# First stage with 1024-wide modulation products, x scaled on ScalarE, and value loads of the linear attention two levels ahead

## Chip, cores and metric

The kernel runs on one core of one Trainium2 chip. The metric is the device time of one execution in microseconds; the median of several executions is compared. Below, PE is TensorE's matmul, DVE is VectorE, ACT is ScalarE, POOL is GpSimd and SP is SyncE, which here only issues DMAs.

## The reference

Two layers of a decoder block run on x of 512 tokens by 1024 features. In each, the normed x is modulated by a vector c, projected once into four groups of heads, each group has its own kind of attention and a gate, and an output projection with a second norm is added back to x.

```python
def hybrid_layer(x, c, ln_pre, ln_post, w_ada, b_ada, w_in, w_out, ...):
    shift, scale, gate = jnp.split(jax.nn.silu(c) @ w_ada + b_ada, 3, axis=-1)
    h = rms_norm(x, ln_pre) * (1.0 + scale[:, None]) + shift[:, None]
    u = split_columns(h @ w_in)
...
    log_a = jax.nn.log_sigmoid(u['c_a'] @ gla_w_a2 + gla_b_a) / GLA_TAU
    o_c = gla_attention(heads(u['c_q'], GROUP_HEADS), heads(u['c_k'], GROUP_HEADS),
                        heads(u['c_v'], GROUP_HEADS), heads(log_a, GROUP_HEADS))
...
    y = mixed @ w_out
    return x + gate[:, None] * rms_norm(y, ln_post)
```

Group C is the gated linear attention: a state per head that decays by a gate and takes up keys times values, token after token.

## The kernel before

All data are float32. For matmuls every operand is split into a high and a low part (whi and wlo of a weight, HH and HL of the activations), and a product is three matmuls: HH with whi, HL with whi, HH with wlo. ACT makes the high part (a cast), DVE the low part (a subtraction). Weights come through tiles wraw (512 KB each); a cast whi (L475) waits for its load.

**The first stage** (`startup`, L659) makes the layer's input and the first two projections. Four tiles of x (128 tokens by 1024) come in, each as two loads of 256 KB. ACT sums the squares of each half (`sq_sum`, L421), DVE and POOL make rstd (`rstd2`: a sum L425 and a power L426), and DVE scales x (L676). Then, for each of the eight groups of 128 features, PE transposes x (`stage`, tp, L703), ACT applies scale and shift (hf, L709; HH, L710), DVE makes HL (L711), and PE multiplies (`mms`, L719 and L723, into a). Scale and shift are made on the fly by `macs` and `mod`: the weight w_mod comes in 32 tiles of 128x512 (256 KB), and DVE multiplies each with silu(c), csr, and sums along the row (L290). Two such products give 128 values, the first one passing on its sum through tmp; four give one group's shift and scale (adass, adags). The string FIRST gives the order of the first loads on SP: x a tile of x, C constants, w a tile of w_mod, P the layer's parameters, T and Q the first weight pieces, c the vector c.

**The linear attention** (`attn_c`, L811) is written as a tree of six levels, 64, 32, 16, 8, 4 and 2 tokens wide. Its values, made by the first projection, are stored to a DRAM buffer vd (L571) and loaded back, once as v (L817) and once per level in another layout as vs (L824): two loads of 128 KB per level, 12 in all, written one behind the other at the start of `attn_c`. Then follow the gate: zp (PE, L830), its logarithm in la (ACT L833 to L835, DVE L836 and L837), the running sum bp (PE, L841), its copy b (ACT, L843) and the steps from there to `level_scores` and `level_values`, level by level, the latter reading vs (L953).

Beside the attentions the rest of the projection runs, and in the background the second layer's modulation (wmod, L290) and the gate of the residual (wada with aac on DVE, L350), whose loads are put on the same SP queue (L282, L387).

**What sets the order.** Each engine works its instructions in a fixed order. A planner sets it when the program is built, from priorities, the order in the code and its own model of when operands are ready; so an edit moves instructions elsewhere too. All DMAs go through SP's one queue. The program has eight DMA semaphores that are used in turn, and a DMA on SP waits until the eighth before it has landed.

Of the kernel before, what the change touches and what calls it, by code (L numbers as in the profile page):

```python
# [20 lines left out]
TLS = False  # L21
B = dict(raw=4, w=3, mx=3, v4=5, dv=2, ad=2, qk=16, g=8, p=3, sz=4, pt=3, sm=4)
QT = QH = QL = QG = 0
QX = 60
FIRST = 'xCwPxwxwxwTQc'
XH = 2
SG, MG = 1, 2
# [154 lines left out]
def pack(inp):  # L182
# [8 lines left out]
    for l in range(DEPTH):  # L191
# [10 lines left out]
        w_gate[l] = wa[:, 2048:].reshape(8, 128, 2, 512).transpose(2, 0, 1, 3)  # L202
        w_mod[l] = wa[:, :2048].reshape(2, 512, 2, 8, 128).transpose(3, 2, 0, 4, 1)
        for i, n in enumerate(('nsa_w1_k', 'nsa_w1_v')):
# [26 lines left out]
def build(tc, A, out_d):  # L231
    nc = tc.nc
    PE, ACT, DVE, POOL, SP = nc.tensor, nc.scalar, nc.vector, nc.gpsimd, nc.sync
    with ExitStack() as ctx:
# [44 lines left out]
        def load_mod(l, n, p, tag):  # L279
# [24 lines left out]
        for ch in FIRST:  # L304
            if ch == 'C':
                SP.dma_start(out=cst[:, 0:256], in_=A['cst'][:, 0:256])
            elif ch == 'w':
                wmods.append(load_mod(0, len(wmods), qk_p, 'qk'))
            elif ch == 'P':
# [229 lines left out]

        def qk_t(name):  # L540
            return qk_p.tile([128, 512], F32, tag='qk', name=name)

# [32 lines left out]

        def qr_t(name):
            return qk_p.tile([128, 512], F32R, tag='qk', name=name)

        def fin_T(l, name, acc):
            par = pars[l]  # L580
            A0, B0 = slice(0, 64), slice(64, 128)
            if name == 'dka':

                kh, kl = qr_t('dkh'), qr_t('dkl')
                for hs in (A0, B0):
# [25 lines left out]
            elif name[0] == 'c':  # L611
                t = qk_t(name)
                ACT.activation(t, acc, AF.Copy, scale=32.0 ** -0.5 if name == 'cq' else 1.0)
                T[name] = t
            elif name[1] == 'q':

                x0, x1 = qr_t('x0'), qr_t('x1')
                ACT.copy(x0[A0], acc[A0])
# [4 lines left out]
            else:  # L623

                k0, k1, l0, l1 = qr_t('k0'), qr_t('k1'), qr_t('kl0'), qr_t('kl1')
                ACT.copy(k0[A0], acc[A0])
# [32 lines left out]
        def startup():  # L659

            tc.cur_priority -= SPX
            for i in range(4):
# [9 lines left out]
                if XF and i == 3:  # L672
                    for c in (slice(0, 128), slice(128, 1024)):
                        DVE.tensor_scalar(x_t[i][:, c], x_t[i][:, c], r, None, op0=ALU.mult)
                else:
                    DVE.tensor_scalar(x_t[i], x_t[i], r, None, op0=ALU.mult)  # L676
            tc.cur_priority += SPX
# [133 lines left out]
        def attn_c(l):  # L811
# [226 lines left out]
        def attn_b(l):  # L1038
# [108 lines left out]
        def wo_piece(l, n):  # L1147
# [218 lines left out]
```

## Time and profile before

| | before |
|---|---|
| median of 3 runs | 694.81 us (694.17 to 696.92) |
| profiled execution, its own time | 697.9 us |
| its span in the profile | 695.7 us |
| TensorE busy | 649.8 us, 93% |
| VectorE busy | 498.6 us, 72% |
| ScalarE busy | 336.8 us, 48% |
| chain that ended last | PE 58%, DVE 17%, DMA 12%, ACT 6% |
| vs<-vd, issue to landing | 24 loads of 128 KB, median 9.8 us |
| wmod<-in_w_mod, issue to landing | 64 loads of 256 KB, median 5.4 us |

The span is the part that the trace covers; the execution's own time is 2.2 us longer. Busy time is what an engine worked, and an engine that is not busy may still be the one that others wait for: the waits tell that. The chain is followed back from the last instruction, at each step to what released it.

### The profile page before, as it was taken

How to read it: one execution, taken by the hardware profiler on the slowest of the kernel's cores; microseconds unless marked ns; L12 is line 12 of the kernel's file. 1: busy time of each engine (PE TensorE's matmuls, PEld its weight loads, DVE VectorE, ACT ScalarE, POOL GpSimd, SP SyncE). 2: the span in 40 equal slices, each digit the busy share in tenths (PEclk: the TensorE clock that was granted, in tenths of full speed). 3: DMA queues.
4: the chain of work that ended last, by engine and by line, in shares of the span. 5: the costliest groups of instructions: out<-in, count | busy, mean ns of one | idle time of the engine just before them, and what ended most of it. 6: DMA issues, size and time to landing. Idle time of an engine off the chain costs nothing.

```text
span 695.7 us, 11980 instructions
## 1 busy us (share of the span) xinstructions
PE 649.8 (93%) x4460; PEld 524.5 (75%) x4460; DVE 498.6 (72%) x1291; ACT 336.8 (48%) x748; POOL 31.1 (4%) x57
## 2 busy tenths in 40 slices
PE   3999889989998999999998989899999999999996
PEld 1797766877777767779996768678777777778895
DVE  5985889666868787784598467743588878768656
ACT  5454444155565555663475244425545436435432
POOL 2000000000001100000012000000000000000000
PEclk9999999999999999999999999999999999999999
DMA  8955764657204444112642681212520021111143
GB/s 299 391 218 166 256 195 138 185 180 272 77 1 138 136 110 133 34 32 81 207 169 79 180 262 43 63 61 91 165 78 32 17 75 32 46 46 46 48 155 116
DMA packets 38163, 87.89 MB, mean 126 GB/s; under 512 B 4185, under 2 KB 7769, under 8 KB 38106
## 3 DMA queue, kind: packets, MB, share of 16 engines
q1 hardware_dynamic: 38106, 87.14, 38.7%
q8 instruction: 35, 0.57, 0.3%
q14 instruction: 22, 0.18, 0.1%
HBM read 81.88 MB, written 5.24 MB: 125 GB/s over the span
## 4 chain that ended last, share of the span: by engine, by line
PE 58%; DVE 17%; DMA 12%; ACT 6%; issue 4%; POOL 1%; SPq 1%; DVEq 0%; POOLq 0%; ACTq 0%
PE mmT L525 19%; PE yo L1169 9%; PE mmTM L536 5%; PE pT L771 5%; DMA wmod<-in_w_mod 4%; PE ob L785 3%; DMA vs<-vd 3%; DVE wlo L478 2%; DMA wraw<-in_w_in 2%; PE a L719 2%; PE yo L1216 2%; PE sc L638 2%; DVE wmod L290 2%; PE od L1007 2%; PE oa L785 2%
## 5 line engine op out<-in xcount | busy, mean ns | idle before, releaser
L525 PE MATMUL mmT<-HH,whi 128*128 128x512 f32 (+1 forms) x352 | 142.8, 406 | 1.4 <-ACT whi L475 1.4
L525 PE MATMUL mmT<-HH,wlo 128*128 128x512 f32 (+1 forms) x352 | 142.6, 405 | 0.4 <-DVE wlo L478 0.4
L525 PE MATMUL mmT<-HL,whi 128*128 128x512 f32 (+1 forms) x352 | 142.3, 404 | 0.0
L757 ACT ACTIVATE p<-p,m 128x256 f32<-128x256 f32 (+3 forms) x128 | 68.8, 538 | 66.9 <-DVE m L755 62.5
L478 DVE TENSOR_TENSOR wlo<-wraw,whi 128x1024 fp32r<-128x1024 f32 (+3 forms) x60 | 72.2, 1205 | 33.2 <-ACT whi L475 32.9
L475 ACT CAST whi<-wraw 128x1024 fp32r<-128x1024 f32 (+3 forms) x60 | 61.5, 1027 | 56.1 <-PE mmT L525 36.8
L525 PEld LDWEIGHTS mmT<-HH,wlo 128*128 128x128 f32 (+1 forms) x352 | 66.2, 188 | 16.1 <-issue 1.5
L525 PEld LDWEIGHTS mmT<-HH,whi 128*128 128x128 f32 (+1 forms) x352 | 66.4, 189 | 15.3 <-ACT whi L475 1.8
L525 PEld LDWEIGHTS mmT<-HL,whi 128*128 128x128 f32 (+1 forms) x352 | 66.4, 189 | 14.0 <-issue 1.2
L771 PE MATMUL pT<-cst,p 128*128 128x128 f32 x296 | 48.9, 279 | 6.0 <-DVE p L768 2.2
L536 PE MATMUL mmTM<-whi,HH 128*128 128x256 f32 (+1 forms) x160 | 48.6, 304 | 3.2 <-ACT HH L467 2.4
L755 DVE CUSTOM_DVE_ANT_0 p<-sc,cst 128x128 f32<-128x128 f32 (+3 forms) x96 | 44.8, 482 | 7.7 <-PE sc L639 7.3
L771 PEld LDWEIGHTS pT<-cst,p 128*128 128x128 f32 x296 | 33.3, 140 | 22.5 <-issue 11.8
L536 PE MATMUL mmTM<-whi,HL 128*128 128x256 f32 (+1 forms) x160 | 47.4, 297 | 0.4 <-DVE HL L468 0.4
L536 PE MATMUL mmTM<-wlo,HH 128*128 128x256 f32 (+1 forms) x160 | 47.2, 295 | 0.0
L1169 PE MATMUL yo<-wlo,HH 128*128 128x256 f32 x144 | 41.9, 291 | 0.0
L1169 PE MATMUL yo<-whi,HH 128*128 128x256 f32 x144 | 41.7, 290 | 0.0
L1169 PE MATMUL yo<-whi,HL 128*128 128x256 f32 x144 | 41.1, 286 | 0.0
L536 PEld LDWEIGHTS mmTM<-whi,HH 128*128 128x128 f32 x160 | 31.0, 194 | 6.1 <-ACT HH L467 3.5
L638 PE MATMUL sc<-k,x 128*128 128x128 f32 (+3 forms) x96 | 32.7, 352 | 0.5 <-DVE m L755 0.2
L778 DVE COPY pt<-pT 128x256 f32<-128x256 f32 (+3 forms) x60 | 28.4, 498 | 6.4 <-PE pT L771 5.5
L536 PEld LDWEIGHTS mmTM<-whi,HL 128*128 128x128 f32 x160 | 30.9, 194 | 1.9 <-DVE HL L468 0.9
(273 smaller groups left out, 1342.2 us busy)
## 6 DMA issues: line engine op xcount, KB each, us to landing
wraw<-in_w_in SPq DMA_DIRECT2D x52, 512.0 KB, 4.1
wmod<-in_w_mod SPq DMA_DIRECT2D x64, 256.0 KB, 5.4
wada<-in_w_gate SPq DMA_DIRECT2D x32, 256.0 KB, 3.1
wor<-in_w_out SPq DMA_DIRECT2D x12, 512.0 KB, 3.3
w<-in_w SPq DMA_DIRECT2D x8, 512.0 KB, 4.7
vs<-vd SPq DMA_DIRECT2D x24, 128.0 KB, 9.8
x<-in_x SPq DMA_DIRECT2D x8, 256.0 KB, 5.2
wor<-in_w_out SPq DMA_DIRECT2D x8, 256.0 KB, 2.9
```

What stands on the lines that cost most here:

```text
L290: DVE.tensor_tensor_reduce(wt, wt, csr[:, 512 * h:512 * h + 512], 0.5, init, ALU.mult, ALU.add, dst)
L475: ACT.copy(hi, raw)
L478: eng.tensor_tensor(out=lo, in0=raw, in1=hi, op=ALU.subtract)
L525: PE.matmul(acc[:m], a, b, start=(n == 0), stop=(n == 23))
L536: PE.matmul(acc[:, :ncol], a, b, start=(n == 0), stop=(n == 23))
L638: PE.matmul(out, q[e][:, qs], k[e][0][:, ks], start=True, stop=False)
L755: DVE.tensor_tensor_reduce(p[:, c], sc[:, c], mask, -0.125, 1e38 if sink is None else sink[0][:, es[j]:es[j] + 1], ALU.add, ALU.min, m[:, ...
L757: ACT.activation(p[:, c], p[:, c], AF.Exp, bias=m[:, j:j + 1], scale=-1.0, accum_out=lsum[:, j:j + 1])
L771: PE.transpose(tp[:, b:b + 128], p[:, b:b + 128], C('ident'))
L778: DVE.tensor_copy(dst, src)
L785: PE.matmul(o[hs, q0:q1], vt[:, kb, vc:vc + 64], PT[:, 512 * kb:512 * kb + q1 - q0], start=(first and kb == 0), stop=(last and kb == 3), s ...
L1169: PE.matmul(acc[:, :n_], a, b, start=(n == 0), stop=(n == last))
```

## The change

It has two parts. In the first stage of layer 0, two tiles of w_mod become one of 128x1024 (512 KB), with one product (L297 of the new kernel) in place of two and no tmp; there are 16 loads and 16 products. The pool of 512-wide tiles (qk, 16) becomes one of 1024-wide tiles (8), in which later users take two tiles at a time (`qk_pair`); kc moves to another pool. x is loaded whole, four loads of 512 KB; one activation of 1024 columns sums the squares (L686), and the scaling of x moves from DVE to ACT (L692). FIRST is another string. In `attn_c`, only levels 64 and 32 of vs are loaded at the start; each later level is loaded two levels ahead, when the scores of the level between have been written.

```diff
-B = dict(raw=4, w=3, mx=3, v4=5, dv=2, ad=2, qk=16, g=8, p=3, sz=4, pt=3, sm=4)
+B = dict(raw=4, w=3, mx=3, v4=5, dv=2, ad=2, qk=8, g=8, p=3, sz=4, pt=3, sm=4)
-FIRST = 'xCwPxwxwxwTQc'
-XH = 2
+FIRST = 'xPwxCxwxwTQwc'
+XH = 1
...
+        def load_mod0(n):
+
+            wt = qk_p.tile([128, 1024], F32, tag='qk', name='wmod')
+            SP.dma_start(out=wt, in_=A['w_mod'][0, n // 2, n % 2].rearrange('a p n -> (a p n)').rearrange('(p n) -> p n', p=128))
+            return wt
+
+        def mod0(n, wt, ss, gs):
+            o, ln, j = _P['bada'][0], _P['lnpre'][0], n // 2
+            DVE.tensor_tensor_reduce(wt, wt, csr, 0.5, pars[0][:, o + n:o + n + 1], ALU.mult, ALU.add, ss[:, n:n + 1])
+            if n % 2:
+                DVE.scalar_tensor_tensor(gs[:, j:j + 1], ss[:, n:n + 1], 1.0, pars[0][:, ln + j:ln + j + 1], op0=ALU.add, op1=ALU.mult)
...
-                    DVE.tensor_scalar(x_t[i], x_t[i], r, None, op0=ALU.mult)
+                    ACT.activation(x_t[i], x_t[i], AF.Copy, scale=r)
...
-                for n in range(4 * j, 4 * j + 4):
+                for n in range(2 * j, 2 * j + 2):
                     if len(wmods) <= n:
-                        wmods.append(load_mod(0, n, qk_p, 'qk'))
-                    mod(0, n, wmods[n], ss, gs)
+                        wmods.append(load_mod0(n))
+                    mod0(n, wmods[n], ss, gs)
...
-            for n, s in enumerate(LEVELS):
+
+            def load_level(n):
+                s = LEVELS[n]
                 vs = vsb[n // 3][:, 512 * (n % 3):512 * (n % 3) + 512].rearrange('p (i a n) -> p i a n', i=4, a=2)
                 vss[s] = vs
                 for e in range(2):
                     SP.dma_start(out=vs[64 * e:64 * e + 64].rearrange('p i a n -> p (i a n)'),
                                  in_=T['cvd'].rearrange('(m w r) e x -> w e m r x', w=2, r=s)[0, e])
+            load_level(0)
+            load_level(1)
...
                 nxt = level_scores(LEVELS[n + 1]) if n + 1 < len(LEVELS) else None
+                if n + 2 < len(LEVELS):
+                    load_level(n + 2)
                 level_values(s, at)
```

The planner's order around the change. First ACT at the start, from the first sum of squares (junk) to the first hf; ct is a step towards csr, whi are the first two weight pieces. Before:

```order
L421 ACTIVATE junk,ss<-x_111 128x512 [waits DMAHW1_49]
L421 ACTIVATE junk,ss<-x_111 128x512 [waits DMAHW2_49]
L337 ACTIVATE ct<-cb 128x512 [waits PE_49]
L421 ACTIVATE junk,ss<-x_119 128x512 [waits DMAHW6_49,DMAHW0_49]
L421 ACTIVATE junk,ss<-x_119 128x512 [waits DMAHW7_49]
L421 ACTIVATE junk,ss<-x_124 128x512 [waits DMAHW1_49,Activation_49]
L421 ACTIVATE junk,ss<-x_124 128x512 [waits DMAHW2_49]
L421 ACTIVATE junk,ss<-x_129 128x512 [waits DMAHW4_49,DVE_49]
L421 ACTIVATE junk,ss<-x_129 128x512 [waits DMAHW5_49]
L475 CAST whi<-wraw 128x996 [waits DMAHW7_49]
L709 ACTIVATE hf_234<-tp,adass,adags 128x512 [waits DVE_49,PE_49]
L475 CAST whi<-wraw 128x1024 [waits DMAHW0_49]
```

After the change:

```order
L686 ACTIVATE junk,ss<-x_111 128x1024 [waits DMAHW1_49]
L353 ACTIVATE ct<-cb 128x512 [waits PE_49]
L692 ACTIVATE x_111<-x_111,rstd 128x1024 [waits Activation_49,Pool_49]
L686 ACTIVATE junk,ss<-x_117 128x1024 [waits DMAHW4_49,DMAHW0_49]
L692 ACTIVATE x_117<-x_117,rstd 128x1024 [waits Activation_49,Pool_49]
L686 ACTIVATE junk,ss<-x_120 128x1024 [waits DMAHW6_49]
L692 ACTIVATE x_120<-x_120,rstd 128x1024 [waits Activation_49,Pool_49]
L686 ACTIVATE junk,ss<-x_124 128x1024 [waits DMAHW0_49,DVE_49]
L692 ACTIVATE x_124<-x_124,rstd 128x1024 [waits Activation_49,Pool_49]
L491 CAST whi<-wraw 128x996 [waits DMAHW2_49]
L491 CAST whi<-wraw 128x1024 [waits DMAHW3_49]
L725 ACTIVATE hf_214<-tp,adass,adags 128x512 [waits DVE_49,PE_49]
```

The scalings of x now stand between the sums of squares, and each waits for POOL's power; the two whi stand ahead of the first hf.

SP's queue in layer 0, from the DMAs just ahead of the loads of vs; wmod is the next layer's modulation and wraw the projection's weights. Before:

```order
L571 DMA vd<-v_tm_c 128x4x128 x2
L282 DMA wmod<-in_w_mod 128x512 x2
L824 DMA vs<-vd 64x512
L817 DMA v_633<-vd 64x4x128 x2
L824 DMA vs<-vd 64x512
L824 DMA vs<-vd 64x1x512 x10
L282 DMA wmod<-in_w_mod 128x512
L487 DMA wraw<-in_w_in 128x1024
L282 DMA wmod<-in_w_mod 128x512
L487 DMA wraw<-in_w_in 128x1024 x4
L282 DMA wmod<-in_w_mod 128x512
```

After the change:

```order
L286 DMA wmod<-in_w_mod 128x512
L842 DMA vs<-vd 64x512
L833 DMA v_575<-vd 64x4x128 x2
L842 DMA vs<-vd 64x512
L842 DMA vs<-vd 64x1x512 x2
L286 DMA wmod<-in_w_mod 128x512 x2
L503 DMA wraw<-in_w_in 128x1024 x2
L286 DMA wmod<-in_w_mod 128x512 x2
L503 DMA wraw<-in_w_in 128x1024
L842 DMA vs<-vd 64x1x512 x2
L503 DMA wraw<-in_w_in 128x1024
```

Behind the first four vs loads now stand two wmod, then two wraw; the other vs loads come later.

DVE in layer 0, from the products of wmod (with their accumulator reads) to the second la of the gate; dkl and dk are a low part of projected keys, x a copy of a projected piece of group B. Before:

```order
L290 ISA wmod,tmp<-wmod,csr,par 128x512 [waits DMAHW1_49]
L290 ISA tmp 128x1
L290 ISA wmod,adass<-wmod,csr,tmp 128x512 [waits DMAHW2_49,DVE_49]
L290 ISA adass 128x1
L587 TENSOR_TENSOR dkl<-mmT,dkh 64x512 [waits Activation_49] x2
L591 COPY ca<-mmT 16x512 [waits Pool_49]
L836 TENSOR_SCALAR la<-zp 128x512 [waits Activation_49]
L610 COPY x_700<-mmT 64x8x31 [waits PE_49]
L837 TENSOR_TENSOR la<-la,t_655 128x512 [waits DVE_49,Activation_49]
```

After the change:

```order
L306 ISA wmod,tmp<-wmod,csr,par 128x512 [waits DMAHW5_49]
L306 ISA tmp 128x1
L601 TENSOR_TENSOR dk<-mmT,dk 64x512 [waits Activation_49] x2
L605 COPY ca<-mmT 16x512 [waits Pool_49]
L306 ISA wmod,adass<-wmod,csr,tmp 128x512 [waits DMAHW4_49,DVE_49]
L306 ISA adass 128x1
L306 ISA wmod,tmp<-wmod,csr,par 128x512 [waits DMAHW5_49]
L306 ISA tmp 128x1
L856 TENSOR_SCALAR la<-zp 128x512 [waits Activation_49]
L624 COPY x_634<-mmT 64x8x31 [waits PE_49]
L857 TENSOR_TENSOR la<-la,t_589 128x512 [waits DVE_49,Activation_49]
```

Two more products, whose loads are the two behind vs, now stand between ca and la.

DVE in layer 1, at ca (the gate's input); aac are products of the residual's gate. Before:

```order
L478 TENSOR_TENSOR wlo<-wraw,whi 128x1024 [waits DMAHW0_49,PE_49,Activation_49]
L478 TENSOR_TENSOR wlo<-wraw,whi 128x1024 [waits DMAHW7_49,PE_49,Activation_49]
L587 TENSOR_TENSOR dkl<-mmT,dkh 64x512 [waits Activation_49] x2
L591 COPY ca<-mmT 16x512 [waits Pool_49]
L350 SCALAR_TENSOR_TENSOR aac<-wada,csil,aac 128x512 [waits DMAHW2_49,DVE_49]
L350 SCALAR_TENSOR_TENSOR aac<-wada,csil,aac 128x512 [waits DMAHW3_49,DVE_49]
L478 TENSOR_TENSOR wlo<-wraw,whi 128x1024 [waits DMAHW4_49,Activation_49]
L836 TENSOR_SCALAR la<-zp 128x512 [waits Activation_49]
```

After the change:

```order
L494 TENSOR_TENSOR wlo<-wraw,whi 128x1024 [waits DMAHW4_49,PE_49,Activation_49]
L494 TENSOR_TENSOR wlo<-wraw,whi 128x1024 [waits DMAHW3_49,PE_49,Activation_49]
L366 SCALAR_TENSOR_TENSOR aac<-wada,csil,aac 128x512 [waits DMAHW6_49,DVE_49]
L366 SCALAR_TENSOR_TENSOR aac<-wada,csil,aac 128x512 [waits DMAHW7_49,DVE_49]
L366 SCALAR_TENSOR_TENSOR aac<-wada,csil,aac 128x512 [waits DMAHW2_49,DVE_49]
L494 TENSOR_TENSOR wlo<-wraw,whi 128x1024 [waits DMAHW0_49,PE_49,Activation_49]
L601 TENSOR_TENSOR dk<-mmT,dk 64x512 [waits Activation_49] x2
L605 COPY ca<-mmT 16x512 [waits Pool_49]
```

Three aac now stand ahead of dk and ca, where before two stood behind ca.

## Rows read from the trace of the kernel before

**Rows 1.** page, part 1 (busy us, share, count) and part 4 (last chain).

```profile
PE 649.8 (93%) x4460; PEld 524.5 (75%) x4460; DVE 498.6 (72%) x1291; ACT 336.8 (48%) x748; POOL 31.1 (4%) x57
...
PE 58%; DVE 17%; DMA 12%; ACT 6%; issue 4%; POOL 1%; SPq 1%; DVEq 0%; POOLq 0%; ACTq 0%
```

**Rows 2.** timeline, ACT, 0 to 20: start, us, line, operation, tiles, [idle <-releaser].

```profile
4.84 0.62 ACT L421 ACTIVATE junk<-x 128x512 f32<-128x512 f32 x1
...
15.25 1.02 ACT L475 CAST whi<-wraw 128x996 fp32r<-128x996 f32 x1 [1.17 <-DMA wraw<-in_w_in]
...
18.74 0.60 ACT L710 CAST HH<-hf 128x512 fp32r<-128x512 f32 x1
```

**Rows 3.** timeline, DVE, 0 to 20 us: the last x scaling.

```profile
15.69 0.75 DVE L676 TENSOR_SCALAR x<-x,rstd 128x1024 f32<-128x1024 f32 x1 [0.44 <-POOL rstd L426]
```

**Rows 4.** timeline, POOL, 0 to 20 us: the last of four powers (rstd).

```profile
14.66 0.99 POOL L426 TENSOR_TENSOR rstd<-rstd,mhalf 128x1 f32<-128x1 f32 x1 [0.99 <-DVE rstd L425]
```

**Rows 5.** waits, PE, 0 to 52 us: waited for, total, times, longest.

```profile
PE tp L703 <- DVE x L676: 8.4, 4, 4.5
...
PE a L719 <- DVE HL L711: 0.7, 1, 0.7
```

**Rows 6.** windows: us, busy (count) by engine, granted PE clock, DMA share, GB/s.

```profile
24.00:28.00 4.00, 4.00 (x14) 3.62 (x13) 4.00 (x13) 2.00 (x4) 0.52 (x1) 1.00 1.05 400
28.00:32.00 4.00, 4.00 (x27) 3.65 (x26) 4.00 (x12) 2.31 (x4) 0.00 (x0) 1.00 1.04 388
76.00:80.00 4.00, 3.61 (x16) 3.12 (x16) 4.00 (x9) 2.09 (x2) 0.00 (x0) 0.61 0.73 264
412.00:416.00 4.00, 2.34 (x9) 2.21 (x10) 3.04 (x5) 1.71 (x5) 0.00 (x0) 0.70 0.95 352
```

**Rows 7.** timeline, PE, 16 to 82 us: first projection matmul, first bp.

```profile
19.39 0.65 PE L719 MATMUL a<-whi,HH 128*128 128x332 f32 x1 [0.43 <-ACT HH L710]
...
67.42 1.05 PE L841 MATMUL bp<-cst,la 128*128 128x128 f32 x8
```

**Rows 8.** timeline, SP queue, 50 to 76 us: DMA issues of layer 0.

```profile
52.31 1.03 SPq L282 DMA_DIRECT2D wmod<-in_w_mod  x2
...
56.08 10.85 SPq L824 DMA_DIRECT2D vs<-vd  x11
...
69.36 0.33 SPq L487 DMA_DIRECT2D wraw<-in_w_in  x1
```

**Rows 9.** timeline, SP queue, 62 to 68 us: the same vs loads, cut later.

```profile
63.17 3.77 SPq L824 DMA_DIRECT2D vs<-vd  x2
...
66.42 0.52 SPq L824 DMA_DIRECT2D vs<-vd  x1
67.77 0.34 SPq L282 DMA_DIRECT2D wmod<-in_w_mod  x1
```

**Rows 10.** timeline, DVE, 52 to 82 us: a product, and the second la.

```profile
57.07 0.75 DVE L290 CUSTOM_DVE_ANT_0 wmod<-wmod,csr,par 128x512 f32<-128x512 f32 x1 [1.60 <-DMA wmod<-in_w_mod]
...
66.55 0.69 DVE L837 TENSOR_TENSOR la<-la,t 128x512 f32<-128x512 f32 x1 [0.79 <-ACT t L835]
```

**Rows 11.** waits, PE, 65 to 82 us.

```profile
PE mmT L525 <- ACT whi L475: 1.4, 1, 1.4
...
PE mmT L525 <- DVE wlo L478: 0.4, 1, 0.4
```

**Rows 12.** timeline, SP queue, 398 to 404 us: DMA issues of layer 1.

```profile
399.16 0.52 SPq L824 DMA_DIRECT2D vs<-vd  x1
...
403.02 0.89 SPq L487 DMA_DIRECT2D wraw<-in_w_in  x2
```

**Rows 13.** timeline, PE, 400 to 410 us: zp of layer 1.

```profile
403.44 1.15 PE L830 MATMUL zp<-par,ca 17*128 17x128 f32 x8
```

**Rows 14.** timeline, ACT, 383 to 424 us: a weight cast.

```profile
407.80 1.05 ACT L475 CAST whi<-wraw 128x1024 fp32r<-128x1024 f32 x1 [5.97 <-DMA wraw<-in_w_in]
```

**Rows 15.** waits, PE, 382 to 424 us.

```profile
PE bp L841 <- DVE la L837: 3.0, 1, 3.0
```

More of the change, by code (lines that the diff above doesn't have):

```diff
@@ L202, in pack @@
         w_gate[l] = wa[:, 2048:].reshape(8, 128, 2, 512).transpose(2, 0, 1, 3)
-        w_mod[l] = wa[:, :2048].reshape(2, 512, 2, 8, 128).transpose(3, 2, 0, 4, 1)
+        if l:
+            w_mod[l] = wa[:, :2048].reshape(2, 512, 2, 8, 128).transpose(3, 2, 0, 4, 1)
+        else:
+            w_mod[l] = wa[:, :2048].reshape(1024, 2, 8, 128).transpose(2, 1, 3, 0).reshape(8, 2, 2, 128, 512)
         for i, n in enumerate(('nsa_w1_k', 'nsa_w1_v')):
@@ L307, in build @@
             elif ch == 'w':
-                wmods.append(load_mod(0, len(wmods), qk_p, 'qk'))
+                wmods.append(load_mod0(len(wmods)))
             elif ch == 'P':
@@ L538, in mm_TM, with qk_pair @@
             return acc
-        def qk_t(name):
-            return qk_p.tile([128, 512], F32, tag='qk', name=name)
+        def qk_pair(name, dt=F32R):
+            t = qk_p.tile([128, 1024], dt, tag='qk', name=name)
+            return t[:, 0:512], t[:, 512:1024]
         T = {}
@@ L574, in fin_tm @@
                     DVE.tensor_scalar(bg, bg, 0.5, 0.5, op0=ALU.mult, op1=ALU.add)
-        def qr_t(name):
-            return qk_p.tile([128, 512], F32R, tag='qk', name=name)
         def fin_T(l, name, acc):
@@ L582, in fin_T @@
             if name == 'dka':
-                kh, kl = qr_t('dkh'), qr_t('dkl')
+                kh, kl = qk_pair('dk')
                 for hs in (A0, B0):
@@ L611, in fin_T @@
             elif name[0] == 'c':
-                t = qk_t(name)
+                if name == 'cq':
+                    T['cqk_'] = qk_pair('cqk', F32)
+                t = T['cqk_'][name == 'ck']
                 ACT.activation(t, acc, AF.Copy, scale=32.0 ** -0.5 if name == 'cq' else 1.0)
@@ L615, in fin_T @@
             elif name[1] == 'q':
-                x0, x1 = qr_t('x0'), qr_t('x1')
+                x0, x1 = qk_pair('x01')
                 ACT.copy(x0[A0], acc[A0])
@@ L623, in fin_T @@
             else:
-                k0, k1, l0, l1 = qr_t('k0'), qr_t('k1'), qr_t('kl0'), qr_t('kl1')
+                (k0, k1), (l0, l1) = qk_pair('k01'), qk_pair('kl')
                 ACT.copy(k0[A0], acc[A0])
@@ L1082, in attn_b @@
             PE.matmul(cp_[:, 64:128], hv, par[:, o:o + w], start=True, stop=True)
-            kct_ = qr_t('kc')
+            kct_ = g_t('kc', [128, 128], F32R)
             kc = [kct_[:, 0:64], kct_[:, 64:128]]
@@ L1155, in wo_piece @@
                     r = raw[:, nc_ * j:nc_ * (j + 1)]
-                    hi, lo = qr_t('wo2h'), qr_t('wo2l')
+                    hi, lo = qk_pair('wo2')
                     ACT.copy(hi, r)
```

## The prediction

> **What bounds the kernel now.** I read the page first: PE is busy 93% of the span and carries 58% of the chain that ended last, VectorE 17% and DMA 12% [rows 1]. So most of the run is a full PE and an edit pays only where PE stands. I then listed PE's waits in the three places that the change touches, and read the engines around each. At the start PE waits 8.4 us for the scaled x [rows 5]; the first projection matmul begins at 19.39 [rows 7]. In layer 0, behind the 12 loads of the linear attention's values (vs), PE waits 1.4 us for a weight cast and 0.4 for its low half [rows 11], since the weight's load was issued only at 69.36 [rows 8]; behind these waits the granted clock is 0.61 over 4 us [rows 6], which with the two levels of 2.4 and 1.2 GHz is 3.1 us at the lower one, so about 1.6 us lost. In layer 1 the same place costs 3.0 us at bp [rows 15]: ScalarE stands 5.97 us for a weight piece [rows 14] and the gate's first activation is queued behind that cast. The granted clock is 0.70 in the stretch of that wait [rows 6], 1.2 us lost.
>
> **First stage: x and the modulation.** Removed from VectorE: four scalings of 0.75 [rows 3] and half the products, 32 of about 0.75 [rows 10] becoming 16 that lie between 0.75 and 1.5 each. That is between 3 us (the scalings alone) and 15 us of VectorE time. I count it at nothing: while the projection runs, PE is full (4.00 of 4 us in each of the stretches shown, [rows 6]) and its one wait for VectorE is 0.7 [rows 5], so that 0.7 is all that could be had.
>
> What costs is the order on ScalarE. Before, ScalarE ran the sums of squares ahead, tile after tile as x landed, and VectorE scaled. Now ScalarE's row is square, scale, square, scale, and a scale waits for its own rstd (VectorE, then a power on POOL), with the next square queued behind it. One round is a square of 1024 (two of 0.62, [rows 2], or some 1.1 as one), the rstd on VectorE (about 0.2), the power of 0.99 [rows 4], and a scaling of about 1.05, taken from the cast of 996 columns, 1.02 [rows 2]: 3.4 us. The first x is in by about 5.4 (its square ran at 4.84, [rows 2]); the first round ends near 8.3, the fourth near 18.5, where before VectorE's last scaling ended at 16.4 [rows 3]. Behind it on ScalarE stand two weight casts of 1.02, which before ran partly while the last x was made, then the two steps from transposed x to HH, 0.7 and 0.60 [rows 2]. First projection matmul: 18.5 + 2.0 + 1.3 = 21.8, against 19.39, so **+2.4**. Bounds: +1.5 if a square and a scale take 0.9 each, +4 if VectorE's product stands before an rstd.
>
> A rule of the Trainium skill speaks against this edit: ScalarE: Activation LUTs, Rules for kernel authors, has plain multiplications go to VectorE, not to ScalarE. Here the row of VectorE (0.75 for 1024 columns) beside the cast of ScalarE (1.02 for 996) agrees. By the formula of the same page (What ACT_TABLE_LOAD costs), 280 ns plus 0.833 ns per column with one pointer operand, a scaling would be an estimated 1.13 us, and the sum 0.3 us later than mine.
>
> Part of the 2.4 comes back. In 24 to 28 PE issues 14 matmuls and in 28 to 32 27, both fully busy [rows 6]: PE runs at the 1.2 GHz level for the first 8.5 us of the projection, though the record of the granted clock reads 1.00, and the 0.7 wait for HL lies inside. Later, after a wait, the lower level lasts about 3.1 us [rows 6]. If the start after the change is denser (HL and the modulation are ready when PE begins), the slow part lies between 3.1 and 8.5 us, so between 0 and some 2.5 us are returned, and the 0.7 wait goes in either case. I take about half: +2.4 - 0.7 - 0.8 = **+0.9**, range -0.8 to +2.5. The larger loads of x and of the modulation are on the path only before the first square; from there on x waits for the chain above and not for DMA.
>
> **Layer 0, the vs loads.** Before, SP issued all 12 in a row, 56.08 to 66.93 [rows 8], because a DMA on SP waits until the eighth before it has landed. The row of vs at 63.17 waited for level 32's first half, the one at 66.42 for its second [rows 9]; the next landings follow 1.35 us later (67.77, [rows 9]). So the two level-32 loads of 128 KB need about 3.3 us each, slower by far than any load of 256 KB beside them, and land one behind the other. Now four vs loads are issued, 64 and 32, and behind them two modulation loads, then weights. The weights come some 5 us earlier than 74 us and the 1.8 us of waits go. But VectorE's row now has two modulation products, which need those two loads, in front of la; before they stood behind it. If everything on the queue lands in the order of issue, as the vs rows do, these two land behind 66.4, at about 67.1 and 67.8 (256 KB at the 390 GB/s of [rows 6] is 0.7 us). Then product (0.75, [rows 10]), la, a copy, the second la: this ends near 70.2, where before it ended at 67.24 [rows 10]. bp, at 67.42 before [rows 7], starts at 70.25: **+2.8**. Against it stand -1.8 for the weight waits; the lower clock behind the old wait (1.6) is replaced by one behind the new. Sum **+1.0**, range -0.6 (no lower clock there) to +2.6 (the lower clock and the weights' low half late as well).
>
> **Layer 1, the same place.** Level 32's second half landed by 399.16 [rows 12]; two weight pieces issued at 403.02 [rows 12] now follow it almost at once, so the 5.97 us on ScalarE go, and with them the 3.0 us at bp and its 1.2 us of clock: -4.2. But VectorE's row has three gate products (aac) in front of ca, where before ca came first. The third needs a load that is queued behind two gate loads and two weight pieces: 2 x 0.25 + 2 x 0.5 + 0.25 MB behind 399.2 at 390 GB/s gives 403.8. Product, a weight's low half, two dk and ca are some 4.4 us more: zp starts at 408.3 instead of 403.44 [rows 13]. PE's row has seven matmuls of 0.23 more in front of it, so PE waits about 3.3, and a lower clock follows again (1.2). bp then comes 5 us behind zp as now, without a wait of size. Sum -4.2 + 3.3 + 1.2 = +0.3 if nothing else moves, -2 if PE has other work; I take **-0.6**.
>
> Elsewhere the planner reorders instructions in small pieces on all engines; PE is full there and I count nothing, +-1. The pool of qk in pairs, kc moved to another pool and the later vs loads (level 16 is issued while level 64's values are multiplied) are counted at nothing, since their readers stand tens of us behind.
>
> **Sum.** +0.9 + 1.0 - 0.6 = +1.3. On the profiled execution (span 695.7 and 2.2 around it, 697.9) this is 699.2; that execution lies 3.1 above the median of 694.8, so on the median **696.1**. Own range of this case: 692.5 to 699.5.
>
> **Rivals.** *The loads don't hold each other.* If the modulation and gate loads land 4.8 us after their issue, as the two issued at 52.31 did (product at 57.07, [rows 8, 10]), the new waits at bp and zp don't arise and both old stalls go: -1.8 - 1.6 in layer 0, -4.2 in layer 1, +0.9 at the start: 694.8 - 6.7 = **688.1**. For it: nothing but the queue ties these loads to vs. Against it: the vs rows landed strictly one behind the other.
> *The start pays in full* (slower): on VectorE a product of 1024 columns stands directly in front of each rstd. If its load lands while ScalarE squares, each round takes up to 0.9 us more; the first projection matmul comes at 24.5, the slow clock lasts the same 8.5 us, and the end of the stage moves by +5.1 - 0.7 = +4.4. With +0.4 of the layers: **699.6**. It decides from a first matmul beyond about 24. Against it: the first modulation load is queued behind the first x and the parameters, so it should be in before the second square.
> *The change does less than it says*: both vs stalls stay, the start too: 694.8, inside same.
>
> **How the numbers follow.** A measurement here tells about 0.5%, 3.5 us, from no change. My forecast 0.43, nearly all of it within 0.5%; loads not held 0.27; the start in full 0.17; nothing moves or small reorderings decide 0.13, one third to each side. Faster: 0.27 + 0.04 + 0.02 = 0.33. Slower: 0.14 + 0.04 + 0.04 = 0.22. Same: 0.45. The range reaches to both rivals: 687.5 to 700.5.
>
> **What would show it.** First projection matmul at 21.8 and the ScalarE row of squares and scales spaced by 3.4; the end of the projection near 52.7; bp of layer 0 with PE idle about 2.8 and VectorE waiting for a modulation load in front of la; no weight wait near 75; layer 1 with PE idle at zp, not at bp. It is wrong if VectorE has its products before 64 (loads not held), or if the squares run ahead on ScalarE, or if PE's clock stays low longer behind the new waits.

## The result: slower by 0.9%

The changed kernel takes 701.59 us (median, 700.52 to 702.52, 4 executions) against 695.21 of the kernel before (4 executions): ratio 1.0089, 95% interval 1.0061 to 1.0117. The forecast was 696.1 with a range up to 700.5, so it missed, and on the side that it held for the least likely. The profiled execution of the changed kernel took 702.37 us (span 700.6), that of before 697.9 (span 695.7); the traces below account for these 4.9 us of span.

The page of the changed kernel, parts 1 and 4, beside [rows 1]:

```profile
PE 646.4 (92%) x4460; PEld 523.8 (75%) x4460; DVE 493.2 (70%) x1255; ACT 340.9 (49%) x744; POOL 28.2 (4%) x57
...
PE 60%; DVE 15%; DMA 10%; ACT 7%; issue 4%; SPq 1%; POOL 1%; DVEq 0%; POOLq 0%; ACTq 0%
```

PE works 3.4 us less than before and VectorE 5.4 less, and the run is longer: what came is waiting, not work. The start of named steps on PE in both traces, before and after, shows where:

| step on PE | before | after | difference |
|---|---|---|---|
| first projection matmul of the first stage | 19.39 | 22.08 | +2.7 |
| first matmul behind the first stage | 51.77 | 51.45 | -0.3 |
| bp, layer 0 | 67.42 | 70.22 | +2.8 |
| kp, behind it in layer 0 | 79.87 | 84.76 | +4.9 |
| steps of layer 0 near 300 us | | | +2.6 |
| zp, layer 1 | 403.44 | 412.04 | +8.6 |
| dS, layer 1 | 427.44 | 432.06 | +4.6 |
| steps near 660 us | | | +4.6 |

**The first stage.** Timeline of ScalarE after the change, 0 to 24 us (start, duration, line, operation, tiles, [idle before it <- what ended it]), which answers to [rows 2 to 4]:

```profile
9.50 1.06 ACT L686 ACTIVATE junk<-x 128x1024 f32<-128x1024 f32 x1 [1.31 <-DMA x<-in_x]
...
11.50 1.15 ACT L692 ACTIVATE x<-x,rstd 128x1024 f32<-128x1024 f32 x1 [0.85 <-POOL rstd L431]
12.56 1.04 ACT L686 ACTIVATE junk<-x 128x1024 f32<-128x1024 f32 x1
...
17.57 1.15 ACT L692 ACTIVATE x<-x,rstd 128x1024 f32<-128x1024 f32 x1 [0.85 <-POOL rstd L431]
```

The row is square, scale, square, scale. It waits 1.31 us for the second x to be loaded; from then on a scale follows the last one after 3.04 us, of which 0.85 us are spent waiting for POOL's power. PE's waits of 0 to 52 us and the counts of matmuls, which answer to [rows 5, 6]:

```profile
PE tp L719 <- ACT x L692: 6.8, 3, 2.3
```

```profile
24.00:28.00 4.00, 4.00 (x22) 3.65 (x21) 4.00 (x8) 2.18 (x3) 0.52 (x1) 1.00 1.03 414
28.00:32.00 4.00, 4.00 (x26) 3.70 (x25) 4.00 (x8) 2.94 (x4) 0.00 (x0) 1.00 1.03 410
68.00:72.00 4.00, 1.78 (x9) 1.78 (x9) 3.87 (x7) 2.34 (x3) 0.00 (x0) 0.68 0.81 254
72.00:76.00 4.00, 4.00 (x16) 3.52 (x15) 1.98 (x5) 3.16 (x5) 0.00 (x0) 0.50 0.82 227
76.00:80.00 4.00, 4.00 (x13) 3.28 (x13) 0.81 (x4) 0.00 (x0) 0.00 (x0) 0.54 0.80 230
408.00:412.00 4.00, 0.00 (x0) 0.00 (x0) 3.31 (x5) 1.62 (x2) 0.00 (x0) 0.85 0.76 257
412.00:416.00 4.00, 3.96 (x13) 3.35 (x14) 2.64 (x4) 2.16 (x4) 0.00 (x0) 0.50 1.04 261
416.00:420.00 4.00, 4.00 (x16) 3.23 (x15) 2.12 (x4) 2.07 (x4) 0.00 (x0) 0.80 0.77 198
```

The columns of the second fence are: stretch, its length, busy time (count) of PE, PE's weight load, VectorE, ScalarE and POOL, granted clock, DMA share, GB/s. In 24 to 28 PE issues 22 matmuls where before it issued 14: by the length of the single matmuls (0.48 us for 332 columns at the 1.2 GHz level, 0.31 above it) that level ends at 25.1 and not at 27.9. From 22.08 to 51.45 PE waits for nothing, where before it waited 0.7 us for HL [rows 5]. So the projection starts 2.7 us later and ends 0.3 us earlier.

**Layer 0.** VectorE's and PE's timeline after the change, which answer to [rows 10] and [rows 7]:

```profile
59.83 0.68 DVE L605 COPY ca<-mmT 16x512 f32<-16x512 f32 x1
67.10 0.75 DVE L306 CUSTOM_DVE_ANT_0 wmod<-wmod,csr,tmp 128x512 f32<-128x512 f32 x1 [6.59 <-DMA wmod<-in_w_mod]
67.77 0.08 DVE L306 DVE_READ_ACCUMULATOR2_ANT adass<- 128x1 f32 x1
...
69.49 0.67 DVE L857 TENSOR_TENSOR la<-la,t 128x512 f32<-128x512 f32 x1
```

```profile
70.22 2.07 PE L861 MATMUL bp<-cst,la 128*128 128x128 f32 x8 [4.07 <-DVE la L857]
...
81.06 1.16 PE L923 MATMUL oc<-cst,vdg 128*128 128x128 f32 x8 [0.71 <-DVE vdg L888]
83.73 0.50 PE L541 MATMUL mmT<-HH,whi 128*128 128x512 f32 x1 [1.50 <-ACT x L622]
```

VectorE stands idle for 6.59 us in front of the second modulation product, whose load was issued at 57.6 and lands at 67.1; la ends at 70.16 and bp follows at 70.22, with PE idle for 4.07 us. The clock falls while PE still waits: 0.68, 0.50 and 0.54 in the three stretches from 68 to 80 (windows above) are 10.2 us at the 1.2 GHz level, and in windows of 0.5 us they run from 69.5 to 79.7. The first of these windows, and one of layer 1, in the same columns:

```profile
69.50:70.00 0.50, 0.00 (x0) 0.00 (x0) 0.50 (x2) 0.50 (x2) 0.00 (x0) 0.50 1.02 381
411.00:411.50 0.50, 0.00 (x0) 0.00 (x0) 0.47 (x2) 0.50 (x1) 0.00 (x0) 0.50 0.94 172
```

PE worked in 9.4 of the 10.2 us, so 4.7 us are lost, where before 3.1 us at that level cost 1.6 [rows 6]. The old waits for a weight near 75 [rows 11] are gone.

While VectorE waits, the DMA engines are first all busy and then nearly idle. Windows of 2 us, the last two columns DMA share and GB/s:

```profile
62.00:64.00 2.00, 2.00 (x10) 1.62 (x10) 0.00 (x0) 1.95 (x3) 0.00 (x0) 1.00 1.06 278
64.00:66.00 2.00, 2.00 (x10) 1.45 (x8) 0.00 (x0) 1.07 (x2) 0.00 (x0) 1.00 0.46 121
66.00:68.00 2.00, 0.15 (x1) 0.00 (x0) 0.90 (x3) 0.00 (x0) 0.00 (x0) 1.00 0.13 51
```

A share of 0.13 is 2 of 16 engines, although two modulation loads and two weights have been issued since 57.6. The single DMA packets in the trace tell what runs there. From 65 to 68.8 two rows of the loads are in flight at a time: the last rows of level 32 up to about 65.8, then, for each of the two engines, 8 rows of the first modulation load (up to 66.5), 8 of the second (up to 67.1) and 8 of each weight. Eight of a load's 128 rows are a sixteenth, one engine's share. So the loads behind level 32 had moved most of their rows by 64.6, on the other engines, and only their shares of the two engines that level 32 used were left to wait behind it. The experiments below test that it is level 32's width that does this.

**Layer 1.** The same two engines' timelines, which answer to [rows 12 to 15]:

```profile
403.62 1.54 DVE L366 SCALAR_TENSOR_TENSOR aac<-wada,csil,aac 128x512 f32<-128x512 f32 x2 [5.85 <-DMA wada<-in_w_gate]
407.46 0.75 DVE L366 SCALAR_TENSOR_TENSOR aac<-wada,csil,aac 128x512 f32<-128x512 f32 x1 [2.30 <-DMA wada<-in_w_gate]
...
411.30 0.69 DVE L605 COPY ca<-mmT 16x512 f32<-16x512 f32 x1
```

```profile
412.04 2.07 PE L850 MATMUL zp<-par,ca 17*128 17x128 f32 x8 [5.48 <-DVE ca L605]
...
420.12 1.06 PE L861 MATMUL bp<-cst,la 128*128 128x128 f32 x8
```

The gate products (aac) wait 5.85 and 2.30 us for their loads, ca follows at 411.30 and zp at 412.04 with PE idle for 5.48 us; bp then follows without a wait. The granted clock is 0.85, 0.50 and 0.80 from 408 to 420 (windows above): 6.8 us at the lower level, from 410.8 to 417.6. For the first 1.3 of them PE still waits, so 2.8 us are lost.

### The profile page after: what moved, and what is told of

It reads as the page before. It is cut to its first block, busy times and chain, and to the rows that moved or that the text cites. A ratio compares the mean times of both kernels' runs of the same rounds, so it can differ in the third digit from the quotient of the medians.

```text
span 700.6 us, 11878 instructions
## 1 busy us (share of the span) xinstructions
PE 646.4 (92%) x4460; PEld 523.8 (75%) x4460; DVE 493.2 (70%) x1255; ACT 340.9 (49%) x744; POOL 28.2 (4%) x57
## 4 chain that ended last, share of the span: by engine, by line
PE 60%; DVE 15%; DMA 10%; ACT 7%; issue 4%; SPq 1%; POOL 1%; DVEq 0%; POOLq 0%; ACTq 0%
PE mmT L541 20%; PE yo L1191 9%; PE mmTM L552 6%; PE pT L787 5%; DMA wmod<-in_w_mod 4%; PE ob L801 3%; DMA wada<-in_w_gate 3%; PE a L735 2%; PE sc L654 2%; DVE wlo L494 2%; PE sc L655 2%; PE yo L1238 2%; PE od L1029 2%; PE oa L801 2%; DVE wmod L306 2%
## 5 line engine op out<-in xcount | busy, mean ns | idle before, releaser
L541 PEld LDWEIGHTS mmT<-HH,wlo 128*128 128x128 f32 (+1 forms) x352 | 66.5, 189 | 14.0 <-issue 0.2
L787 PEld LDWEIGHTS pT<-cst,p 128*128 128x128 f32 x296 | 33.1, 140 | 21.8 <-issue 12.5
L366 DVE SCALAR_TENSOR_TENSOR aac<-wada,csil,aac 128x512 f32<-128x512 f32 x28 | 20.9, 748 | 22.4 <-DMA wada<-in_w_gate 22.2
```

The lines of the kernel that those rows point to most:

```text
L366: DVE.scalar_tensor_tensor(acc, w, csil[:, k:k + 1], acc, op0=ALU.mult, op1=ALU.add)
L541: PE.matmul(acc[:m], a, b, start=(n == 0), stop=(n == 23))
L787: PE.transpose(tp[:, b:b + 128], p[:, b:b + 128], C('ident'))
```

## The experiments

The ratios are those to the kernel before, measured beside each run on the same chip, with 95% intervals.

| run | median, us | ratio | interval |
|---|---|---|---|
| stage_only | 696.64 | 1.0027 | 0.9999 to 1.0055 |
| levels_only | 700.98 | 1.0084 | 1.0054 to 1.0115 |
| wide32 | 687.86 | 0.9896 | 0.9857 to 0.9935 |
| stage_wide32 | 690.68 | 0.9925 | 0.9898 to 0.9952 |
| before_wide32 | 694.11 | 0.9968 | 0.9944 to 0.9992 |
| ahead1 | 689.12 | 0.9894 | 0.9866 to 0.9922 |
| wide32_dve | 685.36 | 0.9849 | 0.9824 to 0.9874 |
| wide32_16_dve | 686.54 | 0.9861 | 0.9836 to 0.9887 |
| no_prod | 705.52 | 1.0120 | 1.0076 to 1.0164 |
| narrow64 | 702.80 | 1.0110 | 1.0079 to 1.0141 |
| narrow64c | 709.12 | 1.0209 | 1.0185 to 1.0233 |
| dve_scale | 701.13 | 1.0107 | 1.0073 to 1.0141 |

### Each part alone

stage_only, against the changed kernel (the loads back in a row at the start of `attn_c`):

```diff
-            load_level(0)
-            load_level(1)
+            for n in range(6):
+                load_level(n)
...
-                if n + 2 < len(LEVELS):
-                    load_level(n + 2)
```

> The first stage of the change alone: 1024-wide products, x loaded whole and scaled on ScalarE, pool in pairs; the 12 vs loads stay in a row as before. Theory (the loss sits behind the four vs loads, not at the start): the projection begins at 22.1 and its end stays near 51.5, bp of layer 0 at about 67, the old weight wait of 1.4 is back, total 694 to 696. Rival (the start or the reordered engines cost it): 699 to 702.

Measured 696.64, a little above the first of the two ranges and well below the second; the ratio is 1.0027, with an interval that just holds 1. levels_only is the other half: the kernel before with `load_level` and its calls as in the change.

> The vs loads two levels ahead alone, first stage as before. Theory: the two modulation loads behind level 32 land near 67, one of the products stands before la, bp waits and the clock falls, zp of layer 1 waits about 5: total 698 to 702. Rival (the loss belongs to the first stage): 694 to 696.

Measured 1.0084, the whole loss, as expected. VectorE's timeline of it, 55 to 72 us, and PE's bp:

```profile
67.27 0.75 DVE L290 CUSTOM_DVE_ANT_0 wmod<-wmod,csr,par 128x512 f32<-128x512 f32 x1 [5.74 <-DMA wmod<-in_w_mod]
```

```profile
70.92 1.16 PE L844 MATMUL bp<-cst,la 128*128 128x128 f32 x8 [2.19 <-DVE la L840]
```

The load that was issued behind level 32 lands at 67.27, as with the whole change. So the loss belongs to the value loads; the first stage by itself costs between nothing and 0.55%.

### The width of the level-32 loads

A level-32 load reads 2 blocks of 32 rows that are not neighbours, so its outer count is 2; level 64's is 64 rows. wide32 writes the blocks as loads of their own, 64 KB each:

```diff
-                    SP.dma_start(out=vs[64 * e:64 * e + 64].rearrange('p i a n -> p (i a n)'),
-                                 in_=T['cvd'].rearrange('(m w r) e x -> w e m r x', w=2, r=s)[0, e])
+                    src = T['cvd'].rearrange('(m w r) e x -> w e m r x', w=2, r=s)[0, e]
+                    if s in (32,):
+                        for m in range(64 // s):
+                            SP.dma_start(out=vs[64 * e + s * m:64 * e + s * m + s].rearrange('p i a n -> p (i a n)'), in_=src[m])
+                    else:
+                        SP.dma_start(out=vs[64 * e:64 * e + 64].rearrange('p i a n -> p (i a n)'), in_=src)
```

> The whole change, but each level-32 load of 64 rows is written as two of 32 contiguous rows, so that its outer count is 32 and no longer 2; the same bytes, two DMAs more per layer. Theory (a level-32 load runs on two of the 16 DMA engines at 3.3 us each, and loads queued behind it land only after it): the loads now land within 1 us each, the modulation loads by about 62, bp and zp do not wait, total 687 to 692. Rival (the number of bytes, or the eight outstanding DMAs, hold the loads): they land near 67 as before, 699 to 702.

Measured 687.86: the change turns from 0.9% slower into 1.0% faster. VectorE's timeline of wide32, and its windows at the place where the changed kernel had a share of 0.13:

```profile
62.99 0.74 DVE L306 CUSTOM_DVE_ANT_0 wmod<-wmod,csr,tmp 128x512 f32<-128x512 f32 x1
...
64.12 0.73 DVE L306 CUSTOM_DVE_ANT_0 wmod<-wmod,csr,par 128x512 f32<-128x512 f32 x1
...
64.99 0.69 DVE L861 TENSOR_TENSOR la<-la,t 128x512 f32<-128x512 f32 x1
```

```profile
62.00:64.00 2.00, 2.00 (x10) 1.67 (x9) 1.57 (x4) 1.95 (x3) 0.00 (x0) 1.00 0.85 252
66.00:68.00 2.00, 2.00 (x15) 1.78 (x14) 1.59 (x3) 1.45 (x3) 0.00 (x0) 1.00 0.88 251
```

The products run at 62.99 and 64.12 without a wait, bp starts at 65.85, and in 66 to 68 the share is 0.88. In layer 1 the wait at zp falls from 5.5 to 1.3 us:

```profile
PE zp L854 <- DVE ca L605: 1.3, 1, 1.3
```

The Trainium skill, DMA: Bandwidth & Descriptors, Why a DMA increments its semaphore by 16 and not by 1, gives the rule behind this: a DMA from SP uses the largest number of engines up to 16 that divides the slowest dimension of both sides that is not 1, and always the lowest-numbered ones. The rows agree on the number: 2 blocks, a share of 0.13. Which two engines they were no run shows.

The cost was then doubled. narrow64 wrote the level-64 loads as two blocks of 32 rows:

> The whole change, with the suspected cost doubled: the two level-64 loads, whose outer count is 64 rows, are written with an outer count of 2 (two blocks of 32 rows), as level 32's is; the same bytes, the same number of DMAs, and the planner's order is the same. Theory (a load whose outer count is 2 runs on two of the 16 DMA engines and holds what is behind it): level 64 lands 3.3 us apart too, the modulation loads land 5 to 6.6 us later than with the change, near 73, bp of layer 0 starts near 76, zp of layer 1 is 5 later as well: 708 to 716. Rival (the outer count does not decide, it is the order or the bytes): as the change, 700 to 703.

No effect (1.0110 beside the change's 1.0089): the second range and not the first. The two blocks are neighbours in memory, so they make one run of 64 rows; that the program joins them again is how I read the result, and no trace shows it. narrow64c reads the 64 rows in two interleaved halves, which can't be joined:

```diff
+                    if s == 64:
+                        src = src[0].rearrange('(r w) x -> w r x', w=2)
```

> The whole change, with the suspected cost doubled: the two level-64 loads read their 64 rows in two interleaved halves, so that their outer count is 2 like level 32's (the rows arrive in another order, so the attention's values are mixed up; bytes, number of DMAs and order are the same). Theory (a load whose outer count is 2 runs on two of the 16 DMA engines and holds what is behind it): the modulation loads land 5 to 6.6 us later than with the change, near 73, bp of layer 0 starts near 76, zp of layer 1 is 5 later as well: 707 to 716. Rival (order or bytes decide, not the width): 700 to 703.

Measured 709.12, the direction and the lower end of the size. VectorE's timeline, windows and PE's waits of narrow64c:

```profile
71.50 0.75 DVE L306 CUSTOM_DVE_ANT_0 wmod<-wmod,csr,tmp 128x512 f32<-128x512 f32 x1 [9.97 <-DMA wmod<-in_w_mod]
...
73.89 0.67 DVE L860 TENSOR_TENSOR la<-la,t 128x512 f32<-128x512 f32 x1
```

```profile
68.00:70.00 2.00, 0.00 (x0) 0.00 (x0) 0.00 (x0) 0.00 (x0) 0.00 (x0) 1.00 0.13 48
70.00:72.00 2.00, 0.00 (x0) 0.00 (x0) 0.50 (x1) 0.00 (x0) 0.00 (x0) 0.93 0.13 50
```

```profile
PE bp L864 <- DVE la L860: 7.5, 1, 7.5
...
PE zp L853 <- DVE ca L605: 8.5, 1, 8.5
```

The share of 0.13 now lasts to 72, the product comes 4.4 us later than with the change (1.0 of it because the first stage of this run ended later, at 52.47), and the waits at bp and zp grow from 4.1 and 5.5 to 7.5 and 8.5. Two more narrow loads cost 3 to 3.4 us at each place and not the 5 to 6.6 expected. One reason may be that the first half of level 64 is issued 2.5 us ahead of the second half and level 32, so that part of it is over before the others start; no run separates this. With wide32 and narrow64c the theory stands from both sides.

### Taking level 32 out of the way

ahead1 loads each level one level ahead, so that only level 64 stands in front of the modulation loads:

```diff
-            load_level(1)
...
-                if n + 2 < len(LEVELS):
-                    load_level(n + 2)
+                if n + 1 < len(LEVELS):
+                    load_level(n + 1)
```

> The whole change, but each level of vs is loaded one level ahead, so that level 32 is no longer in front of the two modulation loads in layer 0. Theory: these loads land by 61 to 62, no wait at bp, the loss of the change goes; level 32 lands later but before its values are needed, or costs PE up to 2 us there: 688 to 694. Rival (the loss does not hang on level 32 standing in front): 699 to 702.

Measured 689.12, as expected. Its trace is not as clean as its time: the two products run at 61.52 and 62.35, but PE still waits 2.2 us at bp, since the planner put two more products, whose loads come later, in front of the second la. But layer 1 has no wait at zp, and by the ratios (0.9894 and 1.0089) the run is 1.9% shorter than the change.

### The same width without the change, or with half of it

The edit of wide32 was made to stage_only (stage_wide32) and to the kernel before (before_wide32).

> The first stage of the change, all 12 vs loads in a row as before, level 32 written as two loads of 32 rows for each half. Theory: the SP queue gets through the 12 loads about 5 us earlier, the first weight load behind them is issued near 64 in layer 0, the weight wait of 1.4 us goes, and in layer 1 most of the 3.0 us at bp: 688 to 692. Rival (width does not matter): 694 to 696.

> The kernel before with level 32 written as two loads of 32 rows for each half, nothing else. Theory (narrow loads hold what is queued behind them): weight load behind vs issued 5 us earlier, the 1.4 us and 0.4 us of layer 0 and most of the 3.0 us of layer 1 go: 688 to 692. Rival: 694 to 696.

stage_wide32 measured 690.68, as expected; before_wide32 694.11, a gain of only 0.3% where 0.5 to 1% was expected, and a time in the rival's range. In before_wide32 the two old waits are indeed gone, and bp of layer 1 starts at 405.50 and not at 413.66:

```profile
405.50 1.05 PE L845 MATMUL bp<-cst,la 128*128 128x128 f32 x8
...
418.19 0.55 PE L888 MATMUL kp<-cst,kd 128*128 128x128 f32 x3 [0.86 <-DVE kd L884]
```

That is 8.2 us early. But the run was 3.2 us ahead at 400 us and is 3.3 us ahead at 480: what bp won was given back between. VectorE is busy for 9.57 of the 10 us from 410 to 420, and PE has three waits there that it did not have before: 0.86 us at kp (above), 0.46 for vdg and 0.70 for a copy on ScalarE. The rest of the 4.9 us I did not trace. Where PE runs ahead of what feeds it, a wait that goes is not a gain of the same size.

### VectorE's order

no_prod asks whether layer 0's loss goes through the products in front of la. It replaces the loaded tile by one that is there:

```diff
+            if n in (1, 2, 3):
+                DVE.tensor_tensor_reduce(g_t('scr'), cs, cs, 0.0, init, ALU.mult, ALU.add, dst)
+            else:
+                DVE.tensor_tensor_reduce(wt, wt, cs, 0.5, init, ALU.mult, ALU.add, dst)
```

> The whole change with its narrow level-32 loads, but three of the second layer's modulation products in layer 0 are left out in substance: they multiply a tile that is already there (times zero) and not the loaded one, so that VectorE's row keeps its products and none in front of la waits for a load; the loads themselves stay. Theory (the loss in layer 0 goes through VectorE's order: product waits for its load, la behind it, bp behind la): bp of layer 0 starts near 66 without a wait, the long low clock of 68 to 79 goes, layer 1 keeps its wait at zp; 695.5 to 698.5. Rival (the late weight loads alone cost as much): PE waits for a weight cast near 70 instead, 700 to 702.

Measured 705.52, outside both. PE's and VectorE's timeline:

```profile
65.94 1.05 PE L865 MATMUL bp<-cst,la 128*128 128x128 f32 x8
...
75.30 1.86 PE L874 MATMUL dp<-cst,qkd 128*128 128x4 f32 x8 [5.10 <-DVE qkd L871]
```

```profile
65.07 0.69 DVE L861 TENSOR_TENSOR la<-la,t 128x512 f32<-128x512 f32 x1 [0.79 <-ACT t L859]
69.14 0.75 DVE L310 CUSTOM_DVE_ANT_0 wmod<-wmod,csr,par 128x512 f32<-128x512 f32 x1 [3.37 <-DMA wmod<-in_w_mod]
...
74.56 0.68 DVE L871 TENSOR_TENSOR qkd<-cqk 128x512 f32<-128x512 f32 x1
```

bp starts at 65.94 without a wait, as the theory had it. But the planner now puts the next product, and two weights' low halves behind it, in front of qkd; that product's load lands at 69.14, qkd comes at 74.56, and PE waits 5.10 us at dp instead of 4.07 at bp. The wait moved one step down the same chain. So the run shows that a load that is held stops PE through VectorE's order; it doesn't show what layer 0 would cost without that, and the expected gain did not come.

### The start

wide32_dve and dve_scale put the scaling of x back on VectorE, the one with wide loads, the other with narrow:

```diff
-                    ACT.activation(x_t[i], x_t[i], AF.Copy, scale=r)
+                    DVE.tensor_scalar(x_t[i], x_t[i], r, None, op0=ALU.mult)
```

> wide32 with the scaling of x back on VectorE, all else of the change kept. If the short stretch at the lower clock (3 us, where before it was 8.5) comes from a projection that is not interrupted, the projection begins near 20 and ends near 49.5: 684.5 to 687. If it comes from the later start (the clock rises at about the same time whatever the start), it ends near 51.5 again: 687 to 689.

> The whole change with the scaling of x back on VectorE. The first projection matmul comes near 19.6 instead of 22.1. If the start sets the end of the first stage, that end comes 2.5 us earlier and the time is 698 to 700; if what feeds the stage later (VectorE, full in both) sets it, the end moves by under 0.6 us and the time is 700 to 702.

wide32_dve measured 685.36, dve_scale 701.13. In both the projection begins 2.6 us earlier (19.59 and 19.47) and ends only 0.4 and 0.7 us earlier (50.89 and 50.77). In both the 1.2 GHz level lasted only about 3 us (3.4 and 2.8), so the later start is not what shortens it; but the end near 49.5 that I had tied to this did not come. PE's timeline of dve_scale:

```profile
19.47 1.47 PE L735 MATMUL a<-whi,HH 128*128 128x332 f32 x4 [0.31 <-ACT HH L726]
...
28.92 0.66 PE L719 MATMUL tp<-cst,x 128*128 128x128 f32 x4 [0.60 <-ACT hf L725]
```

With the earlier start PE runs into what feeds it: it waits for hf at 28.3 (0.60 us, the row above) and for HL at 38.8 (0.12), where in the changed kernel it waits for nothing. That is part of the 1.9 us that the early start lost again; the rest I did not trace. dve_scale's time lies in the second of its two ranges, and its end moved by 0.7 where under 0.6 was expected there: 701.13 beside 701.59, the scaling on ScalarE costs the change nothing that can be measured. wide32_dve is 2.5 us ahead of wide32, but their intervals overlap, and its trace has only 0.4 us of that at the end of the stage; I don't count it as shown.

wide32_16_dve is wide32_dve with `if s in (32, 16)`.

> wide32_dve (level 32 in loads of 32 rows, x scaled on VectorE) with level 16 also written in loads of 16 rows, four for each half. Theory: level 16 is loaded later, beside few others, and 6 more DMAs per layer go through the queue of eight: between -1 and +2 beside wide32_dve, so 684.5 to 687.5. If level 16's narrow loads (four engines) still held weights behind them: 682 to 684.

Measured 686.54, as expected beside wide32_dve: as they are, with an outer count of 4, level 16's loads cost nothing that the time shows. The best median of the study is wide32_dve's, 1.5% faster than the kernel before (0.9849) and by the ratios 2.4% faster than the change.

## Why the prediction was wrong, point by point

**The start, +0.9: measured -0.3.** The first projection matmul was put at 21.8 and came at 22.08, by luck: two errors cancelled. The rounds were put at 3.4 us and measured 3.04, because POOL's power took 0.55 and not the 0.99 of [rows 4], while the scale took 1.15. And the second x was not there when ScalarE was ready for it, 1.31 us that the prediction put at nothing ("from there on x waits for the chain above and not for DMA"). (The page of the Trainium skill, ScalarE: Activation LUTs, What ACT_TABLE_LOAD costs, gives 1.13 for the scale, nearer than the 1.05 taken from a cast.) The term that was mis-sized is "I take about half" of the clock: the lower level lasted 3.0 us and not 8.5, so about 2.3 us came back where 0.8 stood in the sum (the start is 2.7 later, the end 0.3 earlier, and 0.7 of the 3.0 is the wait for HL, which went as forecast). VectorE's relief was rightly counted at nothing beyond that 0.7: it was PE's only wait for VectorE once the projection ran. How long the clock stays low moves the end in other runs too: in ahead1, with the same first stage, the lower level lasted 4.7 us and the stage ended at 52.53 and not at 51.45. Why the level was shorter stays open. The stage alone is 1.0027 of before.

**Layer 0, +1.0: the right wait, the clock behind it mis-sized.** The modulation loads behind level 32 were put at 67.1 and 67.8, the products ran at 67.10 and 67.77; bp was put at 70.25 and came at 70.22. The order was right, but the price of 0.7 us for each load was right by luck: it was worked out for a whole load at 390 GB/s, and what ran there was a sixteenth of a load on each of two engines, in 0.65 us. The step that failed is the sentence "the lower clock behind the old wait (1.6) is replaced by one behind the new". The lower level behind the new wait lasted 10.2 us and not 3.1 and cost 4.7 us: 3.1 more than counted. The prediction had named this as a sign of being wrong ("if PE's clock stays low longer behind the new waits") and gave it no price. PE's wait itself was 4.07 and not 2.8, because PE got there 1.3 us earlier. With two later waits (0.71 for vdg and 1.50 for a copy on ScalarE, rows above) layer 0 stood at +4.9 at kp. By 300 us 2.3 of that were given back in pieces that I did not trace one by one.

**Layer 1, -0.6: wrong in sign, measured +2.0** (from +2.6 near 300 us to +4.6 near 660). The wait did move from bp to zp as forecast. zp was put at 408.3 and came at 412.04. Of this, 2.8 us is that the loads of vs went out so much later than before, and 0.9 is the third gate load, which I had placed on the queue behind two weights and landing at 403.8. It could not be issued then: it goes into the tile of the first of the products, and SP's row shows it only at 404.40, when the first product was done. SP's row before, then after:

```profile
389.34 10.33 SPq L824 DMA_DIRECT2D vs<-vd  x11
```

```profile
392.16 1.74 SPq L842 DMA_DIRECT2D vs<-vd  x3
...
395.06 0.90 SPq L503 DMA_DIRECT2D wraw<-in_w_in  x2
404.40 0.33 SPq L403 DMA_DIRECT2D wada<-in_w_gate  x1
```

The load was there at 407.46. PE's wait was 5.48 us where 3.3 stood in the sum, and again the clock cost more, 2.8 us where 1.2 stood. The 1.2 us of clock that should go were read too low: in windows of 0.5 us the level before lasted from 413.8 to 417.0, 3.2 us with 1.6 lost, and the stretch of [rows 6] holds only part of it. With the old wait of 3.0 and this 1.6 gone, and 5.5 and 2.8 in their place, the terms add up to +3.7; where the other 1.7 were won back I did not trace.

**Together**: +1.3 was forecast and the traces differ by +4.9 in span, of which by the table the start gave -0.3, layer 0 +2.9 and layer 1 +2.0. The rival that forecast slower was the wrong one: the later start cost nothing in the end. "The loads don't hold each other" fell. wide32, where they don't, took 687.86 where 688.1 was worked out, in part by luck, since that sum had +0.9 for the start. What the range lacked was a slower case for the right mechanism: the same waits with a longer lower clock.

## What to carry to other kernels

Read the share of the DMA engines where an engine waits for a load: here a share near 2/16 over microseconds said that only two engines had work left, and that every load issued behind the narrow one still had its own part on these two to come. The outer dimension of the load decided that, so write a load whose outer count is 2 as two loads; that was worth 1.9% on the changed kernel (ratios 0.9896 against 1.0089), more than either part of the change. When loads are moved on a queue, look at what comes to stand behind the slowest of them, and at which in-order engine will wait for that.

## What the runs showed of the hardware that I had not expected

The time at the lower clock does not follow from the length of the wait in front of it. Behind waits of 1.35 and 0.39 us before the change it lasted 3.4 us (windows of 0.5 us), behind 4.07 us with the change 10.2, behind 5.48 us 6.8, and behind 2.19 us in levels_only there was none: the granted clock is 1.00 from 68 to 80. At the start the same instructions ran at 1.2 GHz for 8.5, 4.3 and 7.6 us in the traces of the kernel before, of levels_only and of before_wide32, and for 2.1 to 5.2 us in eleven traces with the 1024-wide products. What ends it I can't tell from these runs; a forecast of a wait should carry a cost of a few us beside the wait itself.

POOL's power of one column took 0.55 us in the changed kernel each time and 0.99 in three of four before [rows 4]. No run tells why.
